# Latent attention: scores of two key blocks issued together, a third PSUM bank for the guard scores, VectorE and GpSimd in source order

## The chip, the core and the metric

The kernel runs on one core of one Trainium2 chip. The metric is device time of one launch in microseconds (us). A core has five engines that run their own instruction streams and wait for each other through semaphores: TensorE (PE, with its weight loads shown apart as PEld), VectorE (DVE), ScalarE (ACT), GpSimd (POOL) and SyncE (SP), which here issues most of the DMAs. Matmul results land in PSUM, which this kernel uses as eight banks of 128 partitions x 512 fp32.

## The reference, cut to what matters

One decoder layer: an input projection, two attention branches over 2048 tokens, gates, an output projection and a layer norm. The change touches the second branch, multi-head latent attention with 8 heads:

```python
s = (jnp.einsum('bqhd,bkhd->bhqk', qn_b, k_nope)
     + jnp.einsum('bqhd,bkd->bhqk', qr_b, k_rope)) * scale
s = jnp.where((kpos[None, :] <= qpos[:, None])[None, None], s, -jnp.inf)
p = jax.nn.softmax(s, axis=-1)
return jnp.einsum('bhqk,bkhd->bqhd', p, v)
...
b_out = b_out.reshape(bsz, S, B_WIDTH).astype(x.dtype) * jax.nn.silu(b_gate)
```

## The kernel before

The program has three long parts: projections and the dilated branch, then the latent stage, then the output projection with the layer norm.

The latent stage goes through 16 steps, a step being a pair of heads (4) and a chunk of 512 queries (`steps`, chunks from last to first, so 16, 12, 8 and 4 key blocks of 128 keys per step). `attend3(i)` makes one step. For a key block `kb`, `s_` issues for each of the two heads two full matmuls into one PSUM bank (`s<-ql,k`: 128 keys x up to 512 queries, the hi and lo parts of the operands), and then for both heads a third matmul with only 33 rows of operands (`s<-q,k` in the profile, called `k3` below), which adds the rest of the rope part and the negative row maximum. The two `k3` matmuls use rows 0 to 32 and 64 to 96 of the array. ScalarE then takes the exponential from PSUM (`e<-s`). On the four diagonal blocks of a step VectorE first adds the causal mask to 128 columns of the bank (line 1204). `r_` issues the value matmuls (`o<-e,vl`, two passes per head; head 0 writes partitions 0 to 63, head 1 64 to 127, so only 64 columns of the array each), and adds the exponentials to a running sum per head, `ac` (lines 1222 and 1224). Which engine adds is decided by `AD`: VectorE for both heads if `kb % 3 == 1` and in the last three steps, else GpSimd.

The row maxima come from the *guards* (`guard3`): for a coming step, a matmul of queries against keys (`mx<-k,ql`) and a VectorE maximum over its bank (lines 1148 and 1150), in units that TensorE's plan lays between the matmuls: `pe.tick(units)` issues guard units when enough work has gone by. The maximum is transposed on TensorE (`tr`), negated on ScalarE and written by DMA into a row of `q3`.

`chain(stream, 2, True)` orders TensorE: `s_` of two blocks, then `r_` of the two before them; the ticks sit after head 0, after head 1, after `k3` and between the `r_`. `TA`, `TB`, `TC`, `TD` share out the units among these places. `go_on` advances a clock of work units (one unit is a key block with 512 queries; a pair of heads has 34 by the planner's `weight`), and `later(units, f)` makes `f` due on that clock. At a step's end `epilogue` loads the gate `g` and multiplies it with `o`, and `divide` sums `ac` over partitions on TensorE (`l`), copies the sums, spreads them by DMA (`u`, `sums`, `r`), inverts them on VectorE (`u<-u`, line 944) `D1` units after, and multiplies `g` by `r` (line 954) `D2 + D3` units after that. `WOT` sets when the weights and first operands of the output projection are loaded.

PSUM banks: four for `s`, two (`o`) for the value sums, two (`x`) for guards, `l` and `tr`. TensorE and ScalarE are in source order (`Order`, `InOrder`); VectorE and GpSimd are ordered by the scheduler.

Of the kernel before, what the change touches and what calls it, by code (L numbers as in the profile page):

```python
# [36 lines left out]
TA = 0.22  # L37
TB = 0.28
TC = 0.22
TD = 0.25  # L40
K1T = (1.0, 6, 6.0)
WOT = (16, 18.5, 21, 26, 25, 28)
# [4 lines left out]
D1 = 1.5  # L47
# [23 lines left out]
AI = 13  # L71
AD = lambda kb, h, i: kb % 3 == 1 or i >= AI
# [143 lines left out]
def body(ctx, tc, a, out):  # L216
# [642 lines left out]
    dve = nc.vector  # L859
    with ExitStack() as p24:  # L860
# [31 lines left out]
        def chain(stream, g, three=False):  # L892

            stream = list(stream)
            for n in range(0, len(stream), g):
                two = stream[n : n + g]
                for s_, r_, w in two:
                    s_(w)
                    go_on(w)
                left = sum(w for _, _, w in two) * (1 - (TA + TB + TC if three else 2 * T2))  # L900
                k = max(0, len(held) - (0 if three else LAG))
                for i in range(k):
                    held.pop(0)()
                    pe.tick(left * (1 - TD if i else TD) if k == 2 and three else left / k)
                if not k:
                    pe.tick(left)
                held.extend(r_ for _, r_, _ in two)
# [20 lines left out]
        def divide(acc, cols, y, view, i, then):  # L928
# [13 lines left out]

            def invert():
                dve.reciprocal(u, u)
                dma(sp, out=sums[i].rearrange("h (p j) -> (h p) j", j=8), in_=u)
                later(D2, spread)
# [6 lines left out]
            def finish():  # L953
                dve.tensor_mul(view(y), view(y), r if view is flat else strip(r))
                later(D4, then)

            later(D1, invert)

# [172 lines left out]

        def guard3(i):
# [37 lines left out]
        def attend3(i):  # L1170
# [13 lines left out]
            def s_(kb, w):  # L1184
                lo, n = span(kb)
                kc = slice(kb * P, (kb + 1) * P)
                ss = [spsum() for h in range(2)]
                for h in range(2):
                    s = ss[h]
                    pe.matmul(s[:, 0:n], k1[h][:, kc], q1[h][:, lo:512], start=True, stop=False)  # L1190
                    pe.matmul(s[:, 0:n], k2[h][:, kc], q2[h][:, lo:512], start=False, stop=False)
                    if h == 0:
                        pe.tick(w * TA)
                    if h:
                        pe.tick(w * TB)
# [4 lines left out]
                pair = exps()  # L1200
                for h in range(2):
                    e = pair[:, h]
                    if kb >= 4 * Q:
                        dve.tensor_add(ss[h][:, 0:128], ss[h][:, 0:128], msk[:, 512:640])
                    act.activation(e[:, 0:n], ss[h][:, 0:n], AF.Exp, scale=SCALE_B)
                    tiles[kb].append(e)

            def r_(kb):
# [8 lines left out]
                for h in range(2):  # L1217
                    eng = dve if AD(kb, h, i) else nc.gpsimd
# [4 lines left out]
                    elif kb:  # L1223
                        eng.tensor_add(acc[h][:, lo:512], acc[h][:, lo:512], es[h][:, 0:n])  # L1224
                if kb == last:
                    later(EPD, epilogue)

            def epilogue():
                cols = slice(Q * CH, (Q + 1) * CH)
                rows = slice(512 + p * P, 512 + (p + 1) * P)  # L1230
                g = ep.tile([P, 512], F32, tag="g", name="g3", bufs=3)
                dma(sp, out=g, in_=gat[rows, cols])
# [4 lines left out]
            return [(lambda w, kb=kb: s_(kb, w), lambda kb=kb: r_(kb), span(kb)[1] / 512) for kb in range(last + 1)]  # L1237
# [106 lines left out]
        for i, (p, Q) in enumerate(steps):  # L1344
# [10 lines left out]
            chain(attend3(i), 2, True)  # L1355
# [135 lines left out]
```

## Time and profile before

| | us |
|---|---|
| median of 3 runs (range) | 1585.88 (1580.88 to 1587.72) |
| the profiled execution | 1582.05 |
| its span, first to last instruction | 1580.2 |
| TensorE busy in the span | 1497.2 (95%) |
| VectorE, GpSimd, ScalarE busy | 949.9, 596.0, 516.4 |
| latent stage, 935 to 1396 us of the span | 461 |

The profiled execution takes 1.85 us more than its span. Times in rows are counted from the span's start. Instructions overlap in their records (a matmul's record goes on while the next one streams), so the price of an instruction is read here from the distance between the *starts* of neighbours. The chain that ended last goes mostly through TensorE.

### The profile page before, as it was taken

To read this page: it belongs to the slowest core of one execution; us is meant where nothing else is said; L and a number is where in the kernel's file an instruction comes from. 1 tells how busy PE (TensorE), PEld (TensorE's weight loads), DVE (VectorE), ACT (ScalarE), POOL (GpSimd) and SP (SyncE) were. 2 spreads that over 40 slices of the span, in tenths; PEclk is the share of its full clock that TensorE was granted. 3 is DMA by queue.
4 is the path that set the end of the run, shared out by engine and by line. 5 is a ranking of instruction groups with operands and counts; after the bars stand their busy time and mean duration, and the time that the engine had idled before them with its cause. 6 is when DMAs were issued, how large, how long until landed. Compare 5 with 4: busy or idle time off the path is not lost.

```text
span 1580.2 us, 22798 instructions
## 1 busy us (share of the span) xinstructions
PE 1497.2 (95%) x7960; PEld 1041.3 (66%) x7960; DVE 949.9 (60%) x2241; ACT 516.4 (33%) x958; POOL 596.0 (38%) x514
## 2 busy tenths in 40 slices
PE   9999999998999999998787889999899899999997
PEld 6789988876766666675564654555455454468887
DVE  4121125455557776638968877676576576866665
ACT  5330034422311111066554323333233233622222
POOL 6300020234420010157767635344344344444443
PEclk9999999999999999999999999999899899999999
DMA  7451179777653421648568846526326413334442
GB/s 262 166 152 47 41 225 298 245 236 253 226 185 105 128 87 37 149 148 198 129 176 212 216 126 172 145 66 171 100 65 169 102 51 124 114 121 160 160 159 82
DMA packets 146167, 237.33 MB, mean 150 GB/s; under 512 B 28930, under 2 KB 69154, under 8 KB 141602
## 3 DMA queue, kind: packets, MB, share of 16 engines
q1 hardware_dynamic: 140996, 235.08, 50.3%
q8 instruction: 63, 1.03, 0.3%
q10 hardware_dynamic: 5056, 0.79, 0.3%
q14 instruction: 52, 0.43, 0.1%
HBM read 152.68 MB, written 82.94 MB: 149 GB/s over the span
## 4 chain that ended last, share of the span: by engine, by line
PE 43%; DMA 5%; DVE 4%; issue 1%; ACT 1%; POOL 1%; SPq 0%; ACTq 0%; POOLq 0%; DVEq 0%
PE s L174 26%; PE o L174 10%; PE mx L174 5%; DMA u<-ls 2%; PE l L174 1%; DVE ac L1224 1%; DVE m L1148 1%; ACT e L205 1%; DMA sums<-u 0%; POOL more L987 0%; SPq L205 0%; DVE acc L1037 0%; DMA g<-gat 0%; DMA X<-dx 0%; DMA q<-mt 0%
## 5 line engine op out<-in xcount | busy, mean ns | idle before, releaser
L205 ACT ACTIVATE e<-s 128x512 f32<-128x512 f32 (+3 forms) x434 | 213.0, 542 | 332.4 <-PE s L174 205.1
L1224 POOL TENSOR_TENSOR ac<-ac,e 128x512 f32<-128x512 f32 (+3 forms) x158 | 175.1, 1134 | 224.9 <-ACT e L205 170.8
L174 PE MATMUL mm<-xh,wh 128*128 128x512 f32 x544 | 226.6, 417 | 0.0
L174 PE MATMUL mm<-xl,wh 128*128 128x512 f32 x544 | 224.2, 412 | 0.0
L174 PE MATMUL mm<-xh,wl 128*128 128x512 f32 x544 | 224.1, 412 | 0.0
L764 DVE CUSTOM_DVE_ANT_0 mx<-mx,bias 128x256 f32<-128x256 f32 (+1 forms) x384 | 139.9, 380 | 70.3 <-PE mx L174 50.0
L174 PE MATMUL s<-ql,k 128*128 128x512 f32 (+3 forms) x640 | 173.1, 378 | 2.2 <-ACT e L205 1.8
L1148 DVE TENSOR_REDUCE m<-mx 128x1 f32<-128x512 f32 x192 | 130.3, 687 | 55.7 <-PE mx L174 54.2
L174 PE MATMUL s<-wo,mh 128*128 128x512 f32 (+1 forms) x544 | 159.9, 377 | 0.0
L174 PE MATMUL mx<-k,ql 128*128 128x512 f32 (+2 forms) x320 | 133.5, 426 | 19.5 <-DVE m L1148 14.4
L174 PE MATMUL o<-e,vl 128*64 128x512 f32 (+3 forms) x640 | 142.5, 553 | 0.9 <-ACT e L205 0.9
L354 POOL TENSOR_TENSOR wl<-ws,wh 128x1024 fp32r<-128x1024 f32 x16 | 38.4, 2397 | 248.1 <-ACT wh L353 240.4
L174 PEld LDWEIGHTS s<-ql,k 128*128 128x128 f32 x640 | 111.1, 190 | 30.5 <-issue 8.3
L174 PEld LDWEIGHTS mx<-k,ql 128*128 128x128 f32 x320 | 60.4, 192 | 104.5 <-issue 37.7
L174 PEld LDWEIGHTS mm<-xh,wh 128*128 128x128 f32 x544 | 104.7, 193 | 21.1 <-issue 0.8
L174 PEld LDWEIGHTS mm<-xl,wh 128*128 128x128 f32 x544 | 104.7, 192 | 20.4
L174 PEld LDWEIGHTS mm<-xh,wl 128*128 128x128 f32 x544 | 104.8, 193 | 19.9
L174 PEld LDWEIGHTS s<-wo,mh 128*128 128x128 f32 x544 | 100.1, 188 | 19.5 <-issue 0.4
L987 POOL TENSOR_SCALAR_AFFINE_SELECT e<-e 128x512 f32<-128x512 f32 (+2 forms) x90 | 91.9, 1052 | 44.0 <-issue 26.1
L174 PE MATMUL mx<-kh,qz 128*128 128x256 bf16 (+1 forms) x384 | 104.3, 359 | 4.4 <-DVE m L764 3.7
L174 PE MATMUL s<-wo,ml 128*128 128x512 f32 (+1 forms) x272 | 102.5, 377 | 0.0
L1150 DVE CUSTOM_DVE_ANT_0 mx<-mx,mxb 128x128 f32<-128x128 f32 (+3 forms) x128 | 63.2, 496 | 51.4 <-PE mx L174 50.7
(209 smaller groups left out, 2625.9 us busy)
## 6 DMA issues: line engine op xcount, KB each, us to landing
ws<-wi SPq DMA_DIRECT2D x16, 512.0 KB
X<-dx SPq DMA_DIRECT2D x16, 512.0 KB
g<-gat SPq DMA_DIRECT2D x32, 256.0 KB
r<-sums SPq DMA_DIRECT2D x64, 128.0 KB
mixd<-g SPq DMA_DIRECT2D x32, 256.0 KB
k<-bkh SPq DMA_DIRECT2D x16, 512.0 KB
ql<-bqh SPq DMA_DIRECT2D x32, 256.0 KB
mf<-mixd SPq DMA_DIRECT2D x8, 1024.0 KB
```

The costliest lines, as they stand in the source:

```text
L174: self._pin(self.tc.nc.tensor.matmul(out, lhsT, rhs, start=start, stop=stop))
L205: ins = getattr(self.engine, name)(*args, **kwargs)
L354: nc.gpsimd.tensor_sub(l[:, ks], t[:, ks], f32(h[:, ks]))
L764: nc.vector.tensor_tensor_reduce(out=oi, in0=oi, in1=bias[:, e, 256 - n : 256], scale=1.0, scalar=-3.0e38, op0=ALU.add, op1=ALU.max, accum ...
L987: nc.gpsimd.affine_select(out=v, in_=v, compare_op=ALU.is_ge, fill=0.0, base=0, pattern=[[0, v.shape[1]]] + [[sign * x, y] for x, y in pat ...
L1148: dve.tensor_reduce(out=dst, in_=o, op=ALU.max, axis=AX.X)
L1150: dve.tensor_tensor_reduce(out=o[:, 0:n], in0=o[:, 0:n], in1=mxb[:, 512 - n : 512], scale=1.0, scalar=-3.0e38, op0=ALU.add, op1=ALU.max, a ...
L1224: eng.tensor_add(acc[h][:, lo:512], acc[h][:, lo:512], es[h][:, 0:n])
```

## The change

In the latent stage alone:

- `s_` takes two key blocks: eight full matmuls, then the four `k3` matmuls, then the four exponentials. Ticks come only after each head's two full matmuls. `chain3` then issues `r_` of the two blocks before without ticks between.
- The mask of the diagonal blocks is added on TensorE, by a bf16 matmul with the identity over 128 columns, in place of the VectorE addition.
- While a step is past its fourth key block and not at its last, every third guard unit takes its bank from the `o` pair.
- Of the running sums, GpSimd adds head 0 and VectorE head 1, for every block.
- VectorE's instructions of this stage (guards, sums, epilogue) and GpSimd's sums are pinned to the order of the source (`dve`, `pool`).
- The gate is loaded earlier (`load_g`), the inversion is due 4 units after the sums instead of 1.5, and the first operands of the output projection 28 and 30 units after the start of the last pair of heads instead of 25 and 28.

```diff
-WOT = (16, 18.5, 21, 26, 25, 28)
+WOT = (16, 18.5, 21, 26, 28, 30)
-D1 = 1.5
+D1 = (1.5, 4)
-AD = lambda kb, h, i: kb % 3 == 1 or i >= AI
...
-    dve = nc.vector
+    dve, pool = InOrder(tc, nc.vector), InOrder(tc, nc.gpsimd)
...
+        def chain3(stream):
+            for s_, r_ in stream:
+                s_()
+                finish()
+                held.append(r_)
...
-            later(D1, invert)
+            later(D1[view is flat], invert)
...
-                o = xpsum("mx")
+                spare[1] += 1
+                o = ps.tile([P, 512], F32, tag="o", name="mx", bufs=OB) if spare[0] and spare[1] % 3 == 0 else xpsum("mx")
...
-            def s_(kb, w):
-                lo, n = span(kb)
-                kc = slice(kb * P, (kb + 1) * P)
-                ss = [spsum() for h in range(2)]
-                for h in range(2):
-                    s = ss[h]
-                    pe.matmul(s[:, 0:n], k1[h][:, kc], q1[h][:, lo:512], start=True, stop=False)
-                    pe.matmul(s[:, 0:n], k2[h][:, kc], q2[h][:, lo:512], start=False, stop=False)
-                    if h == 0:
-                        pe.tick(w * TA)
-                    if h:
-                        pe.tick(w * TB)
-                for h in range(2):
-                    b = 64 * h
-                    pe.matmul(ss[h][:, 0:n], k3[b : b + 33, kc], q3[b : b + 33, lo:512], start=False, stop=True)
-                pe.tick(w * TC)
...
-                    if kb >= 4 * Q:
-                        dve.tensor_add(ss[h][:, 0:128], ss[h][:, 0:128], msk[:, 512:640])
...
+            def s_(two, ws):
+                if two[0] == last - 3:
+                    load_g()
+                ss = {}
+                for kb, w in zip(two, ws):
+                    lo, n = span(kb)
+                    kc = slice(kb * P, (kb + 1) * P)
+                    for h in range(2):
+                        s = ss[kb, h] = spsum()
+                        pe.matmul(s[:, 0:n], k1[h][:, kc], q1[h][:, lo:512], start=True, stop=False)
+                        pe.matmul(s[:, 0:n], k2[h][:, kc], q2[h][:, lo:512], start=False, stop=False)
+                        if kb >= 4 * Q:
+                            pe.matmul(s[:, 0:128], identb, msk[:, 512:640], start=False, stop=False)
+                        pe.tick(w * 0.5)
+                    go_on(w)
+                for kb in two:
...
+                        pe.matmul(ss[kb, h][:, 0:n], k3[b : b + 33, kc], q3[b : b + 33, lo:512], start=False, stop=True)
...
-                    eng = dve if AD(kb, h, i) else nc.gpsimd
+                    eng = dve if h else pool
...
+                if kb >= 3:
+                    spare[0] = kb != last
...
-            chain(attend3(i), 2, True)
+            chain3(attend3(i))
```

The order on TensorE in the first step, two key blocks (six and seven) and the value matmuls of the two before. `s<-ql,k` is a full score matmul, `s<-q,k` the `k3`, `mx` a guard, `o` a value matmul (`x4` stands for four in a row). Before:

```order
L174 MATMUL s<-q_7962,k_8154 128x512 x2
L174 MATMUL s<-ql,k_8246 128x512
L174 MATMUL s<-ql,k_7765 128x512
L174 MATMUL mx<-k_7863,ql 128x512
L174 MATMUL s<-ql,k_8350 128x512
L174 MATMUL s<-ql,k_7863 128x512
L174 MATMUL mx<-k_7863,ql 128x512
L174 MATMUL s<-q_7962,k_8154 128x512 x2
L174 MATMUL o_8610<-e,vl 64x512 x2
L174 MATMUL mx<-k_7863,ql 128x384
L174 MATMUL o_8610<-e,vl 64x512 x2
L174 MATMUL mx<-k_7863,ql 128x512
```

The same engine at about the same place of the changed program:

```order
L168 MATMUL s<-ql,k_8350 128x512
L168 MATMUL s<-ql,k_7863 128x512
L168 MATMUL mx<-k_7863,ql 128x512
L168 MATMUL s<-ql,k_8246 128x512
L168 MATMUL s<-ql,k_7765 128x512
L168 MATMUL mx<-k_7765,ql 128x512
L168 MATMUL mx<-k_7765,ql 128x128
L168 MATMUL s<-ql,k_8350 128x512
L168 MATMUL s<-ql,k_7863 128x512
L168 MATMUL mx<-k_7765,ql 128x512
L168 MATMUL s<-q_7962,k_8154 128x512 x4
L168 MATMUL o_8613<-e,vl 64x512 x4
```

The `k3` of two blocks stand together, directly ahead of the value matmuls, and the guards have moved in among the full score matmuls.

VectorE at the end of the first step of the second pair of heads, where the sums of the step before (`u`) are inverted. `m<-mx` is a guard's maximum, `ISA` the masked kind with its read-out, `mr` the maximum over a step. Before:

```order
L1150 ISA mx,m_9806<-mx,mxb 128x512
L1150 ISA m_9806 128x1
L1155 TENSOR_REDUCE mr<-m_9806 128x8
L1148 TENSOR_REDUCE m_9997<-mx 128x1 x2
L944 RECIPROCAL u<-u 128x8
L1233 TENSOR_TENSOR g_10036<-o_9653,g_10036 128x512
L1148 TENSOR_REDUCE m_9997<-mx 128x1
L1150 ISA mx,m_9997<-mx,mxb 128x128
L1150 ISA m_9997 128x1
L1148 TENSOR_REDUCE m_9997<-mx 128x1
L1224 TENSOR_TENSOR ac<-ac,e 128x512 x2
```

The same inversion in the changed program:

```order
L199 TENSOR_REDUCE m_9987<-mx 128x1 x3
L199 TENSOR_TENSOR ac<-e 128x512
L199 ISA mx,m_9987<-mx,mxb 128x128
L199 ISA m_9987 128x1
L199 TENSOR_REDUCE m_9987<-mx 128x1 x3
L199 TENSOR_TENSOR ac<-ac,e 128x512 x2
L199 ISA mx,m_9987<-mx,mxb 128x256
L199 ISA m_9987 128x1
L199 TENSOR_REDUCE m_9987<-mx 128x1 x3
L199 ISA mx,m_9987<-mx,mxb 128x384
L199 ISA m_9987 128x1
L199 RECIPROCAL u<-u 128x8
```

Between the same point (the step's maximum `mr`) and the inversion there stood two guard maxima; now there stand twelve and three additions.

## Rows read from the trace of the kernel before

**Rows 1.** Busy us (count) by stretch: PE PEld DVE ACT POOL, clock, DMA share, GB/s

```profile
0.00:935.00 935.00, 878.16 (x5082) 667.69 (x5082) 515.88 (x1287) 303.12 (x508) 315.10 (x276) 0.98 0.57 169
935.00:1396.00 461.00, 442.97 (x2049) 226.74 (x2048) 323.62 (x736) 170.91 (x371) 205.29 (x179) 0.98 0.42 114
1396.00:1580.20 184.20, 176.10 (x832) 146.87 (x832) 110.39 (x218) 42.38 (x79) 75.65 (x60) 0.99 0.41 143
```

**Rows 2.** Timeline of TensorE: start, us, engine, line, operation [idle before <-releaser]

```profile
1064.05 0.39 PE L174 MATMUL mx<-k,ql 128*128 128x512 f32 x1
1064.28 0.63 PE L174 MATMUL s<-ql,k 128*128 128x512 f32 x2
1064.74 0.39 PE L174 MATMUL mx<-k,ql 128*128 128x512 f32 x1
1065.06 0.49 PE L174 MATMUL s<-q,k 33*128 33x512 f32 x2
1065.49 0.74 PE L174 MATMUL s<-ql,k 128*128 128x512 f32 x2
1066.07 0.34 PE L174 MATMUL mx<-k,ql 128*128 128x384 f32 x1
...
1067.46 1.08 PE L174 MATMUL o<-e,vl 128*64 128x512 f32 x4
1068.47 0.49 PE L174 MATMUL mx<-k,ql 128*128 128x512 f32 x1
1068.89 1.08 PE L174 MATMUL o<-e,vl 128*64 128x512 f32 x4
1069.90 0.50 PE L174 MATMUL mx<-k,ql 128*128 128x512 f32 x1
```

**Rows 3.** Timeline of TensorE, eight value matmuls without a break

```profile
994.76 1.94 PE L174 MATMUL o<-e,vl 128*64 128x512 f32 x8
996.63 0.50 PE L174 MATMUL mx<-k,ql 128*128 128x512 f32 x1
```

**Rows 4.** Timeline of TensorE: 128-column scores, and a mask matmul of the dilated branch

```profile
1381.68 0.66 PE L174 MATMUL s<-ql,k 128*128 128x128 f32 x4
1382.27 0.33 PE L174 MATMUL s<-q,k 33*128 33x128 f32 x2
...
905.41 0.39 PE L174 MATMUL s<-msk,identb 128*128 128x512 bf16 x1
905.63 0.38 PE L174 MATMUL s<-X 128*128 128x256 bf16 x2
```

**Rows 5.** Timeline of TensorE and VectorE around two long waits

```profile
1115.95 0.47 PE L174 MATMUL mx<-k,ql 128*128 128x128 f32 x1 [5.19 <-DVE m L1148]
1235.35 0.47 PE L174 MATMUL mx<-k,ql 128*128 128x128 f32 x1 [5.68 <-DVE m L1148]
1114.54 0.20 DVE L944 RECIPROCAL u<-u 128x8 f32<-128x8 f32 x1 [5.96 <-DMA q<-mt]
```

**Rows 6.** Busy us by stretch, after these waits, columns as in rows 1

```profile
1112.60:1122.80 10.20, 6.85 (x15) 2.87 (x17) 4.29 (x9) 1.67 (x4) 2.66 (x2) 0.50 0.26 71
1232.20:1242.40 10.20, 7.05 (x17) 2.87 (x17) 4.30 (x9) 1.09 (x2) 2.81 (x2) 0.50 0.19 55
```

**Rows 7.** Timeline of VectorE and GpSimd: reduces, additions, and two additions that meet

```profile
997.30 1.94 DVE L1148 TENSOR_REDUCE m<-mx 128x1 f32<-128x512 f32 x3
1067.75 1.28 DVE L1224 TENSOR_TENSOR ac<-ac,e 128x512 f32<-128x512 f32 x2
...
1078.61 1.28 POOL L1224 TENSOR_TENSOR ac<-ac,e 128x512 f32<-128x512 f32 x1 [3.33 <-ACT e L205]
1078.74 1.70 DVE L1224 TENSOR_TENSOR ac<-ac,e 128x512 f32<-128x512 f32 x1
```

**Rows 8.** Waits of the latent stage: who for whom, us in total, times, longest

```profile
PEld mx L174 <- DVE m L1148: 27.0, 27, 6.0
...
DVE u L944 <- DMA q<-mt: 12.4, 2, 6.5
```

**Rows 9.** Groups of VectorE in the latent stage: busy, mean ns | idle before

```profile
L1204 DVE TENSOR_TENSOR s<-s,msk 128x128 f32<-128x128 f32 x128 | 32.7, 293 | 4.1 <-PE s L174 3.3
...
L954 DVE TENSOR_TENSOR g<-g,r 128x512 f32<-128x512 f32 x18 | 17.3, 960 | 2.3 <-DMA r<-sums 2.3
```

More of the change, by code (lines that the diff above doesn't have):

```diff
@@ L70 @@
 G2 = 1
-AI = 13
-AD = lambda kb, h, i: kb % 3 == 1 or i >= AI
 WSD = 0b0000
@@ L890, in body, with chain @@
         held = []
-        def chain(stream, g, three=False):
+        def chain3(stream):
[3 more added lines that the diff above has]
+                held.append(r_)
+        def chain(stream, g):
             stream = list(stream)
@@ L899, in chain @@
                     go_on(w)
-                left = sum(w for _, _, w in two) * (1 - (TA + TB + TC if three else 2 * T2))
-                k = max(0, len(held) - (0 if three else LAG))
+                left = sum(w for _, _, w in two) * (1 - 2 * T2)
+                k = max(0, len(held) - LAG)
                 for i in range(k):
                     held.pop(0)()
-                    pe.tick(left * (1 - TD if i else TD) if k == 2 and three else left / k)
+                    pe.tick(left / k)
                 if not k:
@@ L941, in divide @@
             r = ep.tile([P, 512], F32, tag="r", name="r", bufs=2)
+            eng = dve if view is flat else nc.vector
             def invert():
-                dve.reciprocal(u, u)
+                eng.reciprocal(u, u)
                 dma(sp, out=sums[i].rearrange("h (p j) -> (h p) j", j=8), in_=u)
@@ L953, in finish @@
             def finish():
-                dve.tensor_mul(view(y), view(y), r if view is flat else strip(r))
+                eng.tensor_mul(view(y), view(y), r if view is flat else strip(r))
                 later(D4, then)
-            later(D1, invert)
+            later(D1[view is flat], invert)
         def attend(p, d):
@@ L1130, in body @@
         ks, qs = {}, {}
+        spare = [False, 0]
         def guard3(i):
@@ L1182, in span @@
                 return j * 128, 512 - j * 128
[L1184 to L1206 removed]
+            gate = []
@@ new lines, in load_g @@
+            def load_g():
+                gate.append(ep.tile([P, 512], F32, tag="g", name="g3", bufs=3))
+                dma(sp, out=gate[0], in_=gat[512 + p * P : 512 + (p + 1) * P, Q * CH : (Q + 1) * CH])
+            def s_(two, ws):
[14 more added lines that the diff above has]
+                for kb in two:
+                    lo, n = span(kb)
+                    kc = slice(kb * P, (kb + 1) * P)
+                    for h in range(2):
+                        b = 64 * h
+                        pe.matmul(ss[kb, h][:, 0:n], k3[b : b + 33, kc], q3[b : b + 33, lo:512], start=False, stop=True)
+                for kb in two:
+                    lo, n = span(kb)
+                    pair = exps()
+                    for h in range(2):
+                        e = pair[:, h]
+                        act.activation(e[:, 0:n], ss[kb, h][:, 0:n], AF.Exp, scale=SCALE_B)
+                        tiles[kb].append(e)
@@ L1230, in epilogue @@
                 rows = slice(512 + p * P, 512 + (p + 1) * P)
-                g = ep.tile([P, 512], F32, tag="g", name="g3", bufs=3)
-                dma(sp, out=g, in_=gat[rows, cols])
+                g = gate[0]
                 dve.tensor_mul(g, box[0], g)
@@ L1235, in epilogue @@
                                           lambda: dma(sp, out=mixd[rows, cols], in_=g)))
-            return [(lambda w, kb=kb: s_(kb, w), lambda kb=kb: r_(kb), span(kb)[1] / 512) for kb in range(last + 1)]
+            return [(lambda two=(kb, kb + 1): s_(two, [span(x)[1] / 512 for x in two]),
+                     lambda two=(kb, kb + 1): [r_(x) for x in two]) for kb in range(0, last + 1, 2)]
         weight = [4 * Q + 2.5 for _, Q in steps]
```

4 lines of the change are left out of this document (removed).

## The prediction

> **What bounds the kernel now.** I read the busy times by stretch first: the latent stage is 461 us of the 1580.2, TensorE is busy for 442.97 of them, VectorE for 323.62 and GpSimd for 205.29 [rows 1]. So TensorE sets the end there, and the question is what its time consists of. The waits by engine name little that TensorE waits for in the stage; the largest is a guard's weight load behind a guard maximum, 27.0 us over 27 times with one of 6.0 [rows 8]. The rest must lie between its own instructions, which the timeline of TensorE shows by starts [rows 2]. A full matmul of 512 columns takes 0.23 us (1064.05 to 1064.28; two in 0.46 to 1064.74). Where the kind changes, it takes more. The last full one ahead of a `k3` takes 0.32 (1064.74 to 1065.06), 0.09 more. The two `k3`, which start together, take 0.43 (to 1065.49), though one after the other they would stream in the same time as two full ones and side by side in half of it, about 0.22; so 0.21 is lost. The two full ones behind them take 0.58 (to 1066.07) instead of 0.46, 0.12 more. Between value matmuls it is the same: four take 1.01 us, a guard between them 0.42 instead of 0.23, four more 1.01, in all 2.44 (1067.46 to 1069.90); eight without a break take 1.87 [rows 3]. One guard of 0.23 thus costs 0.57 there.
>
> The Trainium skill says so too (TensorEngine Tiling (Array Packing), Key Properties: going from one tiling mode to another drains the engine); it gives no time for it, and the sum goes by the rows.
>
> **The change part by part.** Counted from the order of both programs in this stage.
>
> *Fewer changes of kind.* Before there are 160 entries into `k3`, one per key block; after, 80, one per two blocks. Each entry saved is worth 0.09 + 0.21 = 0.30, in all 24 us. Of the 160 `k3` pairs before, 110 are followed by a full matmul (0.12 each); after, none, for all are followed by value matmuls: 13 us. Guards and transposes ahead of value matmuls, 38 before (0.42 - 0.23 = 0.19 each, 7 us), none after; of these, breaks inside a run of values fall from 22 to 0 (2.44 - 0.42 - 1.87 = 0.15 each, 3 us). The row sums `l` now always stand between full matmuls, which costs about 1 us back. Sum: -46 us.
>
> This rests on the second `k3` pair costing only its streaming, 0.22, because its weights are loaded while the first pair streams. The trace of before never has two pairs in a row. The bounds are 0.22 and 0.43, the distance that a pair has now. I take 0.22: eight value matmuls in 1.87 against four in 1.01 show that in one kind the next four add 0.86, which is their bare streaming [rows 2, 3]. At 0.43 it is 80 x 0.21 = 17 us dearer. The Trainium skill (TensorE: Matmul & The Clock Gate, Step-by-step: what each phase is for) lets a weight load run ahead of a running matmul only where the row groups don't conflict or where it goes to the background buffer. By that rule the second pair, on the same rows as the first, is at 0.22 only through the background buffer; no run here shows that for rows.
>
> *The mask on TensorE.* 128 more matmuls of 128 columns. Four full matmuls of 128 columns take 0.59 up to the `k3`, of which 0.09 is the entry, so 0.125 each; the mask matmul of the dilated branch takes 0.22 for 512 columns, a quarter of which is 0.055 [rows 4]. Bounds 7 and 28 us (0.055 and 0.22); I take 0.12, since a new stationary operand comes with each: +15 us. VectorE loses 128 additions, 32.7 us [rows 9], and the exponentials their wait for them. ScalarE, at 170.91 of 461 us, is covered by TensorE.
>
> *The late inversion.* Twice VectorE stood at the inversion of `u` for 12.4 us in all [rows 8], since the DMA that brings `u` was late (the row names another one of ScalarE's queue, issued next to it); the guard maxima behind it were late with it, and TensorE stood for 5.19 and 5.68 us [rows 5]. After both, TensorE's granted clock was 0.50, that is 1.2 GHz, over 10.20 us, in which it was busy for 6.85 and 7.05 us: half of that, 7 us, is lost besides [rows 6]. Due 2.5 units later (a unit is 461 / 136 = 3.4 us), the inversion comes more than 6 us later than before, past both waits. -18 us.
>
> *VectorE in source order.* This is the cost. A maximum takes 0.65 (three in 1.94), an addition 0.64 (two in 1.28) [rows 7]. VectorE adds one head of each block. In a group of two full blocks with the average 3.5 guard units (281 in 80 groups) that is 5.5 x 0.65 = 3.6 us, in a group that lasts 11.5 x 0.23 for scores and guards, and 0.09, 0.43, 0.22, 1.87 and 0.12: 5.4 us. It fits. But 12 groups have six units: 8 x 0.65 + 0.1 = 5.3 us of 5.95, and the additions of both engines now come at the same time. Where they met before, VectorE's addition began 0.13 after GpSimd's and took 1.70 instead of 0.64: it ended half a us after the other [rows 7]. With 1.06 more, six units need 6.4 us of 5.95. Behind a late addition stand the maxima, and guards have two or three banks, so the guard after next stops TensorE. I charge 0.5 us for each of these 12 groups, 6 us, and 0.5 for each of 16 multiplications by `r`, which met GpSimd too (mean 960 ns [rows 9]): 8 us; with the start of the stage, where the dilated branch's last epilogues are in the same queue, +15. Bounds: 0, if three banks cover it, and 35, if every group loses as much as these 12.
>
> A multiplication by `r` also waits in source order for a DMA, at a fixed 2.5 units (8 us) after the inversion; before, 2.3 us over 18 were such waits [rows 9]. Now the maxima stand behind it. +3 us, bounds 0 and 15. The third bank is part of this term; it is in use from the fourth block on, so two groups per step go without.
>
> *The gate loads and `WOT`.* Off the path, except at the end: the first operand of the output projection is loaded 3 units (10 us) later, and its split on GpSimd ends near the projection's start. +2 us, bounds 0 and 8.
>
> Sum: -46 + 15 - 18 + 15 + 3 + 2 = -29 us. Against the profiled execution's 1582.05 that is 1553 us. That execution was 3.8 us under the median of the three runs, within their spread of 6.8, so I leave it there.
>
> **The rivals.**
>
> *VectorE and GpSimd become the bound.* The Trainium skill (GPSIMD Engine Reference, Specifications) says that GpSimd shares its SBUF interface with VectorE, and that instructions of VectorE with two SBUF inputs contend for it; the 1.70 us fit that. As a mechanism of this kernel: in each of the 80 groups the second addition waits 1.06, 85 us on VectorE, whose 323.62 less 32.7 plus 14 more additions (9) then come to 385 of a stage of some 432, while it still must wait for each group's first guard. TensorE then loses about 0.45 per group instead of in the 12 alone, 36 in place of 15: 1574. For it: the row. Against it: the average group has 1.8 us of slack.
>
> *The second `k3` pair isn't hidden*: +17, 1570. For it: no row shows two in a row.
>
> *No new waits.* Three banks cover everything, the mask takes 0.055: -46 + 7 - 18 = -57, 1525. For it: VectorE has 70% of load. Against it: the six-unit groups.
>
> *Slower.* VectorE in source order stands behind a late DMA again, now at the multiplications by `r` or the inversions, as at 1114.54. Each such wait costs 5.4 on TensorE and 3.5 by the clock, 9 us, there are 32 places, and from the fourth on the gain of 29 is gone; with five, 1582 - 29 + 45 = 1598; with seven, 1616. For it: the DMA that blocked `u` for 6 us also carries `sums` and `r`. Against it: 2.3 us of waits at the 18 multiplications before.
>
> **How the numbers follow.** The forecast, 1553 (1538 to 1566 by its own terms), gets 0.57; contention 0.15; the `k3` pair 0.09; no waits 0.11; slower 0.08. A change of 0.5%, 8 us, is about what can be told from none: faster is under 1574, slower over 1590. Faster: 0.57, 0.11, most of the `k3` case and half of the contention, 0.83. Same: the rest of these, 0.09. Slower: 0.08. The range 1527 to 1575 leaves out the slower case and the lower tail of the one without waits.
>
> **What would show it.** In the profile after: a latent stage of some 432 us; in TensorE's timeline four `k3` from start to next kind in 0.65 (0.86 if the second pair isn't hidden); a mask matmul 0.12 from the next start; no idle of 5 us ahead of a guard and no stretch at clock 0.50 behind one; waits of guards for VectorE of some 20 us, spread over many. Wrong would be additions of VectorE with a mean well over 1 us together with guard waits over 40 us, or one VectorE wait of several us on a DMA.

## The result, and the profile after

The changed kernel takes 1563.37 us (median of 4 runs, 1558.75 to 1565.74); the kernel before, run beside it, 1586.8. The ratio is 0.9862, 95% interval 0.9833 to 0.9892: about 22 us faster. The forecast was 1553 in a range of 1527 to 1575: the sign and the range were right; the gain of 29 was put some 7 us too high, and the time came out 10 us later. The profiled execution took 1558.75 us, its span is 1557.0, 23.2 shorter than before's 1580.2.

Busy us by stretch of the kernel after, cut where the first latent score starts and where the output projection starts; columns as in [rows 1]:

```profile
0.00:929.70 929.70, 878.16 (x5083) 666.46 (x5085) 515.53 (x1288) 303.25 (x508) 319.47 (x276) 0.98 0.58 171
929.70:1372.60 442.90, 421.15 (x2174) 225.89 (x2172) 319.66 (x617) 165.25 (x371) 207.49 (x167) 0.98 0.44 119
1372.60:1557.00 184.40, 176.26 (x834) 147.06 (x832) 113.09 (x220) 42.37 (x79) 77.56 (x62) 0.99 0.42 141
```

Cut in the same way, the latent stage of before takes 460.2 us (935.6 to 1395.8), so the stage gained 17.3. The projection takes as long as before, 184.4. The other 5.9 us lie ahead of the stage, where the instructions of TensorE are the same: in the profiles of the experiments below the first latent score starts anywhere from 928 to 939 us, and kernels with the old and with the new stage are mixed among them (928.9 to 935.6, and 928.4 to 938.9), so these 5.9 are scatter and no effect of the change. The stage's 17.3 are what the change is worth in these two profiles; they lie at the lower end of the interval, which is 17 to 27 us. VectorE's busy time hardly fell (323.62 in [rows 1], 319.66 now), although 128 mask additions left it: its additions to the sums take longer, as shown below.

TensorE's timeline after, a mask matmul with a guard behind it, and a `k3` group up to the next full matmuls, to be read by starts against [rows 2]:

```profile
1031.34 0.23 PE L168 MATMUL s<-msk,identb 128*128 128x128 bf16 x1
1031.38 0.47 PE L168 MATMUL mx<-k,ql 128*128 128x512 f32 x1
1031.69 0.63 PE L168 MATMUL s<-ql,k 128*128 128x512 f32 x2
...
1066.97 0.73 PE L168 MATMUL s<-q,k 33*128 33x512 f32 x4
1067.64 1.94 PE L168 MATMUL o<-e,vl 128*64 128x512 f32 x8
1069.50 0.73 PE L168 MATMUL s<-ql,k 128*128 128x512 f32 x2
```

Four `k3` take 0.67 us up to the values, eight values 1.86. The weights of all four are loaded by 1067.27, while the first pair streams and before the second starts (1067.31); the row of the weight loads:

```profile
1066.97 0.30 PEld L168 LDWEIGHTS s<-q,k 33*128 33x128 f32 x4 [0.25 <-issue]
```

The mask matmul itself takes 0.04 to the next start, but the guard behind it takes 0.31 instead of 0.23: mask and guard 0.35 together, so the mask costs 0.12; over all masks of the stage the median is 0.13.

Waits of the latent stage after (930 to 1373 us): who for whom, us in total, times, longest, against [rows 8]:

```profile
PEld mx L168 <- DVE m L199: 20.6, 36, 1.9
...
PE l L168 <- DVE m L199: 6.6, 9, 1.4
PE mx L168 <- DVE m L199: 6.3, 12, 1.4
...
PE mx L168 <- DMA ql<-bqh: 3.2, 1, 3.2
PE l L168 <- POOL ac L199: 2.9, 1, 2.9
...
PE s L168 <- ACT e L199: 1.1, 3, 0.4
```

No wait for `u` is left on VectorE, and none of 5 us on TensorE [rows 5, 8]. Two shorter ones are new: a guard waits 3.16 us for the load of its queries, and the row sums `l` wait 2.92 us for a last sum of GpSimd, which has splits of the projection's operands queued around it (the sum is that of the third step from the end). Behind both, as behind the old two [rows 6], stands a stretch at half clock (window, busy us as in [rows 1], and clock), in which TensorE loses half of 6.54 and of 6.02 us:

```profile
990.90:997.70 6.80, 6.54 (x22) 2.17 (x23) 1.31 (x3) 2.44 (x5) 2.53 (x2) 0.50 1.06 217
...
1349.30:1356.10 6.80, 6.02 (x19) 1.72 (x20) 0.00 (x0) 3.46 (x7) 6.72 (x7) 0.50 0.35 124
```

And `l` has become a waiter: it takes a bank from the two `x` banks, in which guards have gone just before, and stands for their maxima: in the first 14 steps 13 of their groups come right behind a guard, against 8 before. In VectorE's and GpSimd's groups, the additions of 512 columns now take 1.1 us on average on VectorE and 1.4 on GpSimd, where one of VectorE that meets none takes 0.64 [rows 7] and the mean of before was 0.83:

```profile
L1224 DVE TENSOR_TENSOR ac<-ac,e 128x512 f32<-128x512 f32 x62 | 49.9, 832 | 4.5 <-ACT e L205 4.5
...
L199 DVE TENSOR_TENSOR ac<-ac,e 128x512 f32<-128x512 f32 x84 | 93.7, 1115 | 4.1 <-ACT e L199 0.5
...
L199 POOL TENSOR_TENSOR ac<-ac,e 128x512 f32<-128x512 f32 x84 | 121.1, 1442 | 143.9 <-ACT e L199 141.1
```

### The profile page after: what moved, and what is told of

Same layout as the page of the kernel before. It is cut to its first block, busy times and chain, and to the rows that moved or that the text cites. A ratio compares the mean times of both kernels' runs of the same rounds, so it can differ in the third digit from the quotient of the medians.

```text
span 1557.0 us, 22893 instructions
## 1 busy us (share of the span) xinstructions
PE 1475.6 (95%) x8087; PEld 1039.4 (67%) x8088; DVE 948.3 (61%) x2123; ACT 510.9 (33%) x958; POOL 604.5 (39%) x504
## 4 chain that ended last, share of the span: by engine, by line
PE 40%; DVE 5%; DMA 5%; issue 2%; POOL 2%; ACT 1%; SPq 1%; ACTq 0%; POOLq 0%; DVEq 0%
PE s L168 25%; PE o L168 10%; PE mx L168 4%; DMA u<-ls 2%; DVE m L199 2%; PE l L168 1%; POOL e L990 1%; DVE g L199 1%; SPq L199 1%; DMA ql<-bqh 1%; DMA ql<-bql 1%; ACT e L199 1%; DVE acc L1065 0%; DMA sums<-u 0%; DVE mx L199 0%
## 5 line engine op out<-in xcount | busy, mean ns | idle before, releaser
L199 ACT ACTIVATE e<-s 128x512 f32<-128x512 f32 (+3 forms) x434 | 205.2, 546 | 246.2 <-PE s L168 121.9
L199 POOL TENSOR_TENSOR ac<-ac,e 128x512 f32<-128x512 f32 (+3 forms) x128 | 158.0, 1235 | 161.1 <-ACT e L199 156.0
L168 PE MATMUL s<-ql,k 128*128 128x512 f32 (+3 forms) x640 | 183.5, 384 | 1.2 <-ACT e L199 1.1
L168 PE MATMUL mx<-k,ql 128*128 128x512 f32 (+2 forms) x320 | 122.5, 405 | 16.3 <-DVE m L199 8.2
L168 PE MATMUL o<-e,vl 128*64 128x512 f32 (+3 forms) x640 | 137.8, 553 | 0.0
L199 DVE TENSOR_TENSOR ac<-ac,e 128x512 f32<-128x512 f32 (+3 forms) x128 | 117.6, 919 | 7.1 <-ACT e L199 0.5
L990 POOL TENSOR_SCALAR_AFFINE_SELECT e<-e 128x512 f32<-128x512 f32 (+2 forms) x90 | 100.9, 1151 | 39.1 <-issue 19.2
```

Of the source, the lines that this page charges most:

```text
L168: self._pin(self.tc.nc.tensor.matmul(out, lhsT, rhs, start=start, stop=stop))
L199: ins = getattr(self.engine, name)(*args, **kwargs)
L990: nc.gpsimd.affine_select(out=v, in_=v, compare_op=ALU.is_ge, fill=0.0, base=0, pattern=[[0, v.shape[1]]] + [[sign * x, y] for x, y in pat ...
```

## The experiments

Twelve kernels were run, each beside the kernel before; the ratios are to it, with 95% intervals, and stand against 0.9862 (0.9833 to 0.9892) for the changed kernel. One per cent is 16 us; where two runs are compared, the difference is that of their ratios.

| run | median us | ratio (interval) |
|---|---|---|
| `x1`: after, `k3` per block | 1572.7 | 0.9939 (0.9919 to 0.9960) |
| `x2`: after, mask on VectorE | 1559.13 | 0.9842 (0.9820 to 0.9863) |
| `x3`: after, GpSimd's sums (head 0's) left out | 1552.8 | 0.9808 (0.9793 to 0.9823) |
| `x7`: before, pairs alone | 1597.18 | 1.0081 (1.0065 to 1.0096) |
| `x4`: after, `l` in the `o` bank | 1549.84 | 0.9786 (0.9751 to 0.9820) |
| `x5`: after, scheduler's order | 1608.9 | 1.0159 (1.0122 to 1.0196) |
| `x6`: after, early inversion | 1563.44 | 0.9870 (0.9838 to 0.9903) |
| `x8`: after, two guard banks | 1570.82 | 0.9920 (0.9887 to 0.9952) |
| `z1`: before, late inversion alone | 1586.3 | 0.9990 (0.9966 to 1.0013) |
| `z4`: before, pairs and source order | 1585.19 | 0.9984 (0.9962 to 1.0007) |
| `y1`: `x4` and mask on VectorE | 1552.61 | 0.9777 (0.9743 to 0.9812) |
| `y3`: `y1`, third bank sooner, last sums on VectorE | 1557.13 | 0.9813 (0.9772 to 0.9854) |

**`k3` per block.**

```diff
                 for kb, w in zip(two, ws):
...
                         pe.tick(w * 0.5)
+                    for h in range(2):
+                        b = 64 * h
+                        pe.matmul(ss[kb, h][:, 0:n], k3[b : b + 33, kc], q3[b : b + 33, lo:512], start=False, stop=True)
                     go_on(w)
-                for kb in two:
-                    lo, n = span(kb)
-                    kc = slice(kb * P, (kb + 1) * P)
-                    for h in range(2):
-                        b = 64 * h
-                        pe.matmul(ss[kb, h][:, 0:n], k3[b : b + 33, kc], q3[b : b + 33, lo:512], start=False, stop=True)
```

> The changed kernel, but each block's two k3 matmuls stand right behind that block's own full ones again; mask, third bank, orders stay. Theory (entries into k3 cost 0.30 and leaving for a full one 0.12, and TensorE's own time decides): 80 more entries of 0.30 and 80 more exits of about 0.12 come back, 34 us, less what its waits for guards shrink when TensorE goes slower (at most some 10): 1585 to 1598, ratio to the kernel before 1.000 to 1.007. Rival (the gain came from other parts: the inversion moved later and VectorE relieved of the mask): the time stays within 8 us of the changed kernel, ratio 0.986 to 0.991.

Between the two: 12 us come back, not 34. The single pairs cost what [rows 2] say again. TensorE's timeline of this run, one block:

```profile
1067.97 0.39 PE L168 MATMUL mx<-k,ql 128*128 128x512 f32 x1
1068.29 0.50 PE L168 MATMUL s<-q,k 33*128 33x512 f32 x2
1068.72 0.73 PE L168 MATMUL s<-ql,k 128*128 128x512 f32 x2
1069.29 0.40 PE L168 MATMUL mx<-k,ql 128*128 128x512 f32 x1
```

0.32 into the pair, 0.43 for it, 0.57 for the two full ones behind. But the waits fell, since VectorE has more time beside a slower TensorE (waits of this run's stage, as above):

```profile
PEld mx L168 <- DVE m L199: 12.7, 23, 2.2
...
PE l L168 <- DVE m L199: 1.2, 4, 0.3
```

Summed over the stage, start-to-start distances beyond bare streaming that belong to a change of kind are some 27 us more than in the changed kernel, and waits and half-clock stretches some 12 less; the stage is 458.2 us long, 15 more (in a profiled run that took 8 us more than this kernel's median). So pairing the `k3` saves some 27 us of TensorE's time, and about two fifths of this are given back at once, mostly in waits for VectorE.

**The mask on VectorE.**

```diff
-                        if kb >= 4 * Q:
-                            pe.matmul(s[:, 0:128], identb, msk[:, 512:640], start=False, stop=False)
...
                         e = pair[:, h]
+                        if kb >= 4 * Q:
+                            dve.tensor_add(ss[kb, h][:, 0:128], ss[kb, h][:, 0:128], msk[:, 512:640])
```

> The changed kernel, but the mask is added by VectorE to the scores in PSUM again instead of by TensorE. Forecast's size (0.12 us for a mask matmul): 15 us of TensorE go, VectorE gets 32.7 us in source order back, and the exponentials of masked blocks wait for it; net between -10 and +10 us, 1553 to 1573. By the trace after (0.04 to 0.05 us for a mask matmul): only some 6 us of TensorE go, and the masks, queued on VectorE in source order behind guard maxima and additions, hold up the exponentials and with them the values: 5 to 20 us slower than the changed kernel, ratio 0.990 to 1.000. If the mask matmul cost what was forecast and VectorE has room, it is faster than the changed kernel, ratio under 0.983.

About 3 us faster by the ratios, though the intervals overlap; the profiled stage is 7.6 us shorter (435.3). The first expectation held. The second rested on the 0.04 us to the next start and overlooked what the next matmul loses. TensorE's waits for scores' banks grow from 1.1 to 5.1 us:

```profile
PE s L168 <- ACT e L199: 5.1, 11, 0.7
```

**No sums on GpSimd.**

```diff
-                    if kb == 1:
+                    if not h:
+                        if kb == 1:
+                            pool.memset(acc[h], 1.0)
+                    elif kb == 1:
```

> The changed kernel without the row sums of head 0 in the latent stage (GpSimd only fills that sum with ones once per step), so that VectorE's additions have no addition of GpSimd beside them. It leaves out part of the computation, and measures what GpSimd's additions cost the others. Theory A (VectorE is late because its additions meet GpSimd's and take 1.5 instead of 0.65 us): VectorE's 512-column additions all take about 0.65, the guards' and row sums' waits on TensorE for VectorE (some 30 us now) fall to 10 or less, and the long wait of l for a sum of GpSimd at the end of the stage (3 us and 3 more by the clock) goes: 20 to 28 us faster than the changed kernel, ratio 0.968 to 0.974. Theory B (VectorE is late by its order and number of instructions, the meeting hardly matters): only the wait at the end goes, 3 to 8 us, ratio 0.981 to 0.985.

Some 9 us faster than the changed kernel by the ratios, at the border of theory B and far from A. VectorE's 512-column additions fell from 1115 to 747 ns, 31 us in all, and TensorE's waits for VectorE did not follow. VectorE's group and the waits in this run:

```profile
L199 DVE TENSOR_TENSOR ac<-ac,e 128x512 f32<-128x512 f32 x84 | 62.7, 747 | 4.1 <-ACT e L199 0.5
```

```profile
PEld mx L168 <- DVE m L199: 18.7, 35, 1.3
...
PE l L168 <- DVE m L199: 6.5, 10, 1.4
```

The wait of `l` for GpSimd (2.9 us, and about 3 by the clock behind it) is gone, by the two profiles some 6 of the 9 us. So the meeting of the two engines makes VectorE busier, mostly where it has room. GpSimd's own load went with its sums, so the run can't tell the meeting of additions from GpSimd being late by itself; at the wait of `l` it is the latter.

**Pairs alone, in the kernel before.** The edit is `s_`, `chain3` and the list of pairs as in the change, with the mask additions left on VectorE.

```diff
-            chain(attend3(i), 2, True)
+            chain3(attend3(i))
```

> The kernel before with one thing of the change: the latent scores of two key blocks together, their four k3 matmuls behind all eight full ones. The mask stays on VectorE, guards keep two banks, VectorE and GpSimd keep their own order and the old division of the sums, the inversion stays early. Theory (the fewer changes of kind are the gain, 46 us by the forecast): most of it shows even alone, 25 to 46 us less than before, less waits that two banks and later exponentials bring: ratio 0.972 to 0.990. Rival (grouping needs the other parts: with two banks, masks on VectorE and exponentials that come only at the group's end, TensorE waits give back most of it): ratio 0.992 to 1.010.

13 us slower: the rival, at the slow end of its range. TensorE's changes of kind fell, by some 26 us, and waits and half-clock stretches took their place, from some 26 to over 70 (waits of this run's stage):

```profile
DVE u L951 <- DMA u<-ls: 38.2, 9, 8.9
...
PE mx L174 <- DVE m L1155: 19.0, 21, 5.6
...
DVE ac L1234 <- ACT e L205: 17.1, 21, 2.1
...
DVE ac L1232 <- ACT e L205: 10.3, 6, 2.2
```

VectorE stands 38 us for `u` and 27 for exponentials. In before these are the waits (935 to 1396 us) that answer to them, beside the 12.4 in [rows 8]:

```profile
DVE ac L1224 <- ACT e L205: 5.9, 10, 0.8
...
DVE ac L1222 <- ACT e L205: 2.5, 6, 0.5
```

In pairs, exponentials come four at a time at a group's end, and the scheduler had laid additions and inversions ahead of the maxima. What held up the maxima can be read from the trace, guard by guard: between the end of a guard's record and the start of its maximum, VectorE spent 41 us of this stage in additions and 23 idle ahead of an inversion, but less than 1 idle for exponentials. So the 27 us of waits for exponentials are a sign of the order, and not themselves what the guards waited for.

**The scheduler's order, in the changed kernel.**

```diff
-    dve, pool = InOrder(tc, nc.vector), InOrder(tc, nc.gpsimd)
+    dve, pool = nc.vector, nc.gpsimd
```

> The changed kernel, but VectorE and GpSimd are not held to the source's order in the latent stage; the scheduler orders them as in the kernel before. Everything else stays (pairs, mask on TensorE, third bank, late inversion). Forecast's theory (source order costs some 15 us, additions ahead of maxima): faster than the changed kernel by 5 to 15 us, ratio 0.977 to 0.983. Rival (source order costs nothing, or helps because masks and sums come when TensorE needs them): within 3 us or slower, ratio 0.986 to 1.000.

47 us slower than the changed kernel and 25 slower than before. The rival had the sign, but its range ended at 1.000: with the rest in place the source's order is no cost but, of the parts taken back one by one, the one worth most. The waits of this run, and a piece of VectorE's timeline with TensorE's next guard:

```profile
DVE ac L1242 <- ACT e L199: 55.1, 46, 4.8
...
PEld mx L168 <- DVE m L1154: 37.9, 39, 2.3
...
PE mx L168 <- DVE m L1154: 23.6, 24, 1.9
PEld mx L168 <- DVE m L1156: 20.3, 18, 5.3
...
DVE u L947 <- DMA u<-ls: 13.8, 5, 4.6
```

```profile
1260.20 0.20 DVE L947 RECIPROCAL u<-u 128x8 f32<-128x8 f32 x1 [4.57 <-DMA u<-ls]
1260.32 0.68 DVE L1242 TENSOR_TENSOR ac<-ac,e 128x512 f32<-128x512 f32 x1
1260.91 0.29 DVE L1156 CUSTOM_DVE_ANT_0 mx<-mx,mxb 128x128 f32<-128x128 f32 x1
...
1261.31 0.79 PE L168 MATMUL mx<-k,ql 128*128 128x512 f32 x1 [4.83 <-DVE m L1156]
```

The inversion, due 4 units late in the source, still stands ahead of the maximum, waits 4.57 us for its DMA, and TensorE's next guard waits 4.83 for the maximum. The due time moved it in the source; the scheduler laid it where it wanted. Counted as for `x7`, finished guards stood behind additions for 98 us of this stage and behind idle time ahead of inversions for 17; in the changed kernel it is 5 and 0.

**The late inversion**, taken back in the changed kernel (`x6`) and done alone in the kernel before (`z1`).

```diff
-D1 = (1.5, 4)
+D1 = (1.5, 1.5)
```

> The changed kernel with the inversion of the row sums due after 1.5 units again instead of 4. Forecast's theory (an early inversion stands on VectorE for a late DMA, the maxima wait behind it, TensorE loses 5.4 us and 3.5 more by the clock at each of two places): 10 to 25 us slower than the changed kernel, ratio 0.992 to 1.002, with one or two waits of 4 us or more on VectorE for u's DMA and a stretch at a granted clock of 0.50 behind each. Rival (with the other orders the DMA is in time, or the third bank covers it): within 4 us, ratio 0.984 to 0.989.

```diff
-WOT = (16, 18.5, 21, 26, 25, 28)
+WOT = (16, 18.5, 21, 26, 28, 30)
-D1 = 1.5
+D1 = (1.5, 4)
...
-            later(D1, invert)
+            later(D1[view is flat], invert)
```

> The kernel before with one thing of the change: the inversion of the latent row sums due after 4 units instead of 1.5 (and, since the last results come later with it, WOT as in the change). Forecast's theory (the two waits of VectorE for u's DMA cost 18 us, clock included): 12 to 20 us faster than before, ratio 0.987 to 0.993. Rival, after the run in which the inversion was put back without a loss (each such stall costs its 5 us only where nothing else is late, and where the scheduler orders VectorE a due time moves little): within 6 us of before, ratio 0.996 to 1.004.

Neither makes a difference (0.9870, 0.9990); both rivals were right. VectorE's wait in `z1`, and in `x6`:

```profile
1239.48 0.20 DVE L944 RECIPROCAL u<-u 128x8 f32<-128x8 f32 x1 [6.85 <-DMA u<-ls]
```

```profile
1121.54 0.20 DVE L199 RECIPROCAL u<-u 128x8 f32<-128x8 f32 x1 [2.36 <-DMA u<-ls]
```

Alone, the later due time leaves the waits for `u` as long as they were (14.8 us in three; before, 12.4 in two [rows 8] and 2.2 in two short ones), and it does not even move the inversion: from the end of `l` to its start the median is 3.5 us before and 3.5 in `z1`, but 6.6 in `x6` and 12.3 in the changed kernel. In the source's order even the early inversion waits 2.36 at most, and nothing shows of it in the time.

**Two banks for guards.**

```diff
-                o = ps.tile([P, 512], F32, tag="o", name="mx", bufs=OB) if spare[0] and spare[1] % 3 == 0 else xpsum("mx")
+                o = ps.tile([P, 512], F32, tag="o", name="mx", bufs=OB) if False else xpsum("mx")
```

> The changed kernel without the third PSUM bank for guards; the orders of all engines are the same. Theory (VectorE's order is late in bursts and the third bank covers it): TensorE's waits for guard maxima grow from some 30 us to 45 or more, 12 to 25 us slower than the changed kernel, ratio 0.994 to 1.002. Rival (two banks are enough, as VectorE has 70% of load): within 4 us, ratio 0.984 to 0.989.

Between the two: 9 us slower, with the intervals just overlapping. Guard waits rose, from 20.6 and 6.3:

```profile
PEld mx L168 <- DVE m L199: 33.5, 64, 1.8
...
PE mx L168 <- DVE m L199: 10.1, 20, 1.4
```

**Pairs and source order, in the kernel before.** The edits of `x7`, and `dve` and `pool` pinned as in the change.

```diff
-    dve = nc.vector
+    dve, pool = InOrder(tc, nc.vector), InOrder(tc, nc.gpsimd)
...
-                    eng = dve if AD(kb, h, i) else nc.gpsimd
+                    eng = dve if AD(kb, h, i) else pool
```

> The kernel before with two things of the change: pairs of blocks, and VectorE and GpSimd in the source's order in the latent stage. The mask stays on VectorE, guards keep two banks, the sums their old division, the inversion stays early. Theory (in pairs the scheduler's order puts additions ahead of maxima whose scores are there, and the source's order cures it; these two are the core of the change): 10 to 30 us faster than before, ratio 0.981 to 0.994, and VectorE's waits for exponentials at additions under 10 us against some 47 with pairs in the scheduler's order. Rival (the third bank, the division of the sums and the mask on TensorE are needed to take up the bursts): no faster than pairs alone, ratio 1.000 to 1.010.

Neither quite: 1% faster than pairs alone, and no faster than before. VectorE no longer waits for `u` or for exponentials (this run differs from `x7` by the order alone, so it is the order that took these waits away), but guards still wait more than in the changed kernel, and the old division of the sums makes the two engines wait for each other:

```profile
POOL ac L205 <- DVE ac L205: 115.5, 29, 9.5
...
PE mx L174 <- DVE m L205: 20.6, 22, 4.1
...
DVE g L205 <- DMA g<-gat: 8.3, 4, 3.4
...
DVE ac L205 <- POOL ac L205: 5.7, 4, 1.7
```

From here to the changed kernel another 1.2% is won by what is left. The third bank is 9 us of it by `x8`; the late inversion and the mask add nothing by `x6` and `x2`. What the earlier gate load and one engine per sum are worth was not tried apart and stays open; the row of `g` has VectorE wait 8.3 us for the gate, a wait that the changed kernel does not have in this stage's steps. Nor was the source's order tried in single blocks.

**`l` in the bank of the values.**

```diff
-            l = xpsum("l")
+            l = ps.tile([P, 512], F32, tag="o", name="l", bufs=OB) if view is flat else xpsum("l")
```

> The changed kernel with one edit: the row sums l of the latent stage take the PSUM bank that the previous values left (the third guard bank, which is not yet in use then) instead of one of the two guard banks. Theory (in the trace of the changed kernel l waits 10.5 us over 15 times behind a guard maximum that holds its bank, and this is time of the end): 6 to 10 us faster than the changed kernel, ratio 0.980 to 0.983. Rival (the guards behind l meet the same busy VectorE a little later and wait in its place): within 3 us of the changed kernel, with more wait at the guards in the trace.

12 us faster than the changed kernel, 2.1% faster than before. The wait of `l` for maxima fell from 6.6 to 0.6 and the guards' did not rise (waits, then busy us of the stage, columns as in [rows 1]):

```profile
PEld mx L168 <- DVE m L199: 19.9, 33, 1.7
...
PE l L168 <- DVE m L199: 0.6, 2, 0.4
```

```profile
932.90:1362.60 429.70, 415.58 (x2173) 224.35 (x2171) 318.67 (x618) 165.19 (x371) 206.85 (x166) 1.00 0.45 122
```

The stage is 13.2 us shorter; 6 of these are `l`'s own waits, and the granted clock of the stage is 1.00 against 0.98: of the two stretches at half clock, in which the changed kernel lost 3.3 and 3.0 us, only half of the second is left, which is some 5 more. That the bank took the stretches away is not shown: `x6`, with `l` in the old bank, has the same wait of `l` for GpSimd (2.92 us) and full clock behind it (window, busy us and clock as above):

```profile
1359.40:1366.20 6.80, 6.80 (x38) 2.97 (x40) 2.44 (x6) 3.73 (x8) 6.72 (x6) 1.00 0.27 80
```

The gain itself rests on six runs and not on this profile.

**Two combinations.** `y1` has the edits of `x4` and `x2`; `y3` besides takes the third guard bank from a step's second block on, and adds all sums of the last two steps on VectorE:

```diff
-                if kb >= 3:
-                    spare[0] = kb != last
+                if kb:
+                    spare[0] = kb != last and Q > 0
...
-                    eng = dve if h else pool
+                    eng = dve if h or i >= 14 else pool
```

> The changed kernel with two edits: the row sums l of the latent stage in the bank that the values left (12 us faster by itself), and the mask added by VectorE instead of TensorE (3 us faster by itself). If they add up: 14 to 18 us faster than the changed kernel, ratio 0.974 to 0.978. Rival (without l's waits VectorE's masks come on the path, as scores then wait for later exponentials): no faster than with the bank alone, ratio 0.978 to 0.983.

> The changed kernel with four edits: row sums l in the bank that the values left, the mask on VectorE, the third guard bank from the second block of a step on instead of the fourth (not in the steps of four blocks), and all row sums of the last two steps on VectorE. Theory (the waits of guards after guards at the steps' starts, 4 us, and the wait for GpSimd's last sums, 3 us and 3 by the clock, go): 5 to 9 us faster than the version with the first two edits, ratio 0.969 to 0.974. Rival (VectorE, with masks and more sums, is later at the end): within 3 us of that version or slower.

`y1` is level with `x4` (0.9777, 0.9786) and stands where the ranges of its two expectations meet, so whether the two gains add up isn't settled; `y3` is no faster. The wait of `l` for GpSimd is still there in `y3`, because the edit missed it: GpSimd's last sum, for which `l` waits, ends at 1336.33 us and belongs to the third step from the end, and the edit moves those of the last two. The scores wait more:

```profile
PE s L168 <- ACT e L199: 8.3, 11, 3.1
...
PE l L168 <- POOL ac L199: 3.3, 1, 3.3
```

The best version is `x4`, or `y1`, which can't be told from it; both beat the changed kernel.

## Why the prediction was right in sign, and where its steps failed

**Fewer changes of kind (-46).** Right in mechanism, about 10 too large. The second `k3` pair is hidden: four take 0.67 from start to next kind, forecast 0.65. Against 2 x (0.09 + 0.21) before, a group costs 0.09 to 0.12 into `k3` and 0.24 beyond streaming now; 80 groups save about 20 us, not 24. The term that failed is the 13 us for the 110 `k3` pairs with a full matmul behind them: in the trace of before only 77 of these have two or more full matmuls behind them, with 0.105 lost up to the second one (8 us). The other 33 stand before a lone guard, row sums or a transpose; 13 of them before a guard ahead of values, whose loss was counted again there. Nor do the row sums now stand between full matmuls: in the first 14 steps all of them stand directly ahead of the `k3`. By all transitions in both traces the changes of kind take some 35 us less, the masks set aside: the 27 that `x1` puts back, and the 7 of guards ahead of values.

**The rule on draining.** The trace of `x1` shows it again: a pair of `k3` between full matmuls costs 0.43, against 0.34 from the first pair to the second in the changed kernel, where no kind changes. The Trainium skill (TensorEngine Tiling (Array Packing), Key Properties), by which a change of tiling mode drains the engine, agrees. The second pair takes 0.33 up to the values, although the kind changes there: its weights were loaded before it started, those of the first pair and of a lone one only at the start. By these three prices a load is worth some 0.10 and the change behind a pair some 0.09, as an estimate.

**The mask (+15).** Right by the rows: 0.12 each, 128 times. Taken back, it gave only some 3 us by the ratios and 7.6 in the profiled stage. Scores then waited 4 us more and VectorE was busy for 342.5 us in place of 319.7; that this accounts for the rest is likely, and not shown.

**The late inversion (-18).** Failed as a step. The two waits are gone, as foretold, but not by the due time: alone it leaves them (`z1`), and without it they are gone all the same (`x6`). It was the order of VectorE: `x7` waits 38 us for `u`, and `z4`, which differs from it by the order alone, not at all.

**VectorE in source order (+15).** Failed in sign, where the blocks are paired. I costed it from the number of instructions and the meeting additions, against an order of before that I took to be free. Unpinned, the same program is 47 us slower (`x5`); pinning the paired blocks of `x7` wins 15 (`z4`). In single blocks the order of the scheduler was tolerable: VectorE waited 8.4 us for exponentials, against 27 in `x7` and over 55 in `x5`, and finished guards stood behind additions for 34 us, against 41 and 98. That the maxima stand behind late additions, the fear of this step, is what the change avoids (5 us).

**The sum of the waits.** The three terms on waits (-18, +15, +3) came to 0. By the distances in the traces, waits and half-clock stretches of TensorE together are 26 us before and 29 after, +3. So their sum was nearly right while two of the three reasons were wrong: the old long waits, 11 us and 7 of clock, went, and `l`'s bank, guards at the start of steps, a late query load and GpSimd's last sum took their place. The changes of kind at -35, the mask at +15 and the waits at +3 give -17; the stage shows -17.3. That the whole time came within 10 us of the forecast is in part luck: the two profiles differ by 5.9 us ahead of the stage, where nothing was changed.

**The rivals.** Contention was there (additions of VectorE 1115 ns), but not as the bound: `x3` takes it away and wins some 9 us, more than half of it at one wait at the end of the stage. The Trainium skill (GPSIMD Engine Reference, Specifications) has the two engines share their way to SBUF; `x3` agrees with it on VectorE's time, 1115 against 747 ns, and shows that the time went elsewhere in the kernel. The slower rival, a late DMA on VectorE, did not come about in the source's order; in the scheduler's (`x7`) it did, with 38 us. One argument for it was wrong by the kernel: `u` is loaded through ScalarE's queue, `sums` and `r` through SyncE's. What would have shown me wrong, a mean addition well over 1 us together with guard waits over 40, came true by half: 1.1 us, but 20.6 at the weight loads and 6.3 at the matmuls.

## What to carry to other kernels

Regrouping matmuls to spare changes of kind also regroups everything that feeds on them; the gain stays only if the engines behind are ordered anew for the new rhythm, so test the regrouping and the order together, not the regrouping alone. A due time in the source means something only on an engine that is held to the source's order, as the inversion showed here. After such a change look for short-lived users of a shared PSUM bank that have become waiters: moving the row sums to a bank that lay idle was worth half as much as the whole change.

## What was not expected of the hardware

- A bf16 matmul of 128 columns between float32 ones takes 0.04 us to the next start, and the next one 0.08 more than its usual 0.23: its price is in its neighbour's row.
- Behind stalls of about 3 us, TensorE's granted clock was 0.50 (1.2 GHz) for 6.8 us in the changed kernel; in `x4`, with a stall of 2.93 us at the same place, the 6.8 us behind it show 0.75 on average, and in `x6`, with 2.92 us there, 1.00. The length of the stall did not decide it.
- In the changed kernel, additions of 512 columns with one of the other engine beside them for at least nine tenths of their record take 1.49 us on VectorE (mean of 35) and 1.45 on GpSimd (mean of 29); with nothing of the other engine beside them it is 0.67 (mean of 7) and 1.28 (mean of 12).
